# Both conv-FFN layers: other queues for the operand pieces, and layer 1's last six channel tiles by seven products for output tiles 0 to 3

## The chip, the cores and the metric

One core of a Trainium2 chip runs the whole program. Engines named below: TensorE (PE; PEld is its weight load), VectorE (DVE), ScalarE (ACT), GpSimd (POOL) and SyncE (SP, which only issues transfers here). The metric is the device time of one execution in microseconds; several executions are timed and their median is given.

## The reference

Two layers on x of 1024 tokens x 1024 features in float32, then a last RMS norm with a gain. Only the mixer differs between the layers:

```python
for layer in range(2):
    hn = rms_norm(h, norm_mix[layer])
    h = h + (retention_deltanet_mixer if layer == 0 else rglru_mixer)(hn, ...)
    h = h + conv_ffn(rms_norm(h, norm_ffn[layer]), w_up, conv_w, conv_b, w_down)
return rms_norm(h, norm_final)

def conv_ffn(hn, w_up, conv_w, conv_b, w_down):       # D_FF = 2816 = 22 x 128
    up = causal_dwconv(hn @ w_up, conv_w) + conv_b     # 3 taps, 5632 channels
    gate, val = jnp.split(up, 2, axis=-1)
    return (jax.nn.silu(gate) * val) @ w_down
```

## The kernel before, in words

**Precision.** Each float32 factor is split into a high part (rounded on ACT, a CAST) and a low part (the remainder, a subtraction on DVE). A product of a 128x128 weight tile is three matmuls, high x high, high x low, low x high (`mm3`, L319 to L321). Weights come as float32 halves (`raw`, L292) and are split at L272 (ACT) and L273 (DVE).

**H** is the state: eight tiles H[0..7] of 128 features x 1024 tokens, kept in SBUF.

**FFN up** makes 22 hidden channel tiles p = 0 to 21 (`hidden`), a pair of blocks of outputs at a time by seven products instead of eight (`pair_products`; operands o = 0 to 6 are sums and differences of blocks of tokens and channels). **FFN down** uses the same form. Its 22 channel tiles are three sets: c = 0 has tiles 0 to 7, c = 1 has 8 to 15, c = 2 has 16 to 21. In a set the tiles k and k + depth make a pair (depth 4, 4 and 3). A set runs over t = 0 to 3, the pairs (2t, 2t+1) of output tiles, and over the seven products o; one product is depth x 3 matmuls of 512 columns, 12 in sets 0 and 1 and 9 in set 2. `pair_added` adds each product to H on DVE (L820).

**The operands of FFN down.** When tile p is done, `store_parts` writes its share of the seven operands to DRAM. Operands in `whole` are stored already split (to `pf_dram`, high and low, L880; DVE makes the low part at L878). The others go unsplit to `sf_dram` (L881, L906). For the second tile of a pair the first one's blocks are read back first (L894, L895). `load_set(c, o)` brings an operand in: a split one straight to its place in the operand buffers (L914, 2 x depth transfers), an unsplit one to a piece of `room` (R and three t tiles) at L922, depth transfers, after which ACT (L924) and DVE (L925) split it to its place. Every transfer here is 256 KB and is issued by SP, in the order in which the scheduler places them; an engine's queue goes strictly in order, so a transfer that waits for its data holds those behind it. In set 0 of layer 0, operands 0, 1 and 3 are stored split, in the other sets 5 too. The loads of set 0 are issued while tile 21's up products run, the loads of set c + 1 behind the products of t = 3 of set c, as the table `following` (or `plain`) says. Tile 20's hidden work runs beside tile 21's up products; tile 21's runs inside set 0, behind t = 2.

**Layer 1** has only sets 0 and 1. Tiles 16 to 21 are stored split, whole (`lf_dram`), are read back in set 1, and are multiplied plainly in `final`: 8 output tiles x 6 channel tiles x 3 matmuls, over three cuts of the tokens (512, 256 and 256 columns). Their weights are loaded and split once and kept (`load_kept`). After each output tile of a cut its square is added up (L407, L411) for the last norm. The norm of the first 512 tokens runs beside (`norm_beside`: sums through DRAM and POOL to a row in R); those of the second and third cut on TensorE (`norm_tok` L480, POOL's power at L472, `norm_row` L489). `scale` multiplies H with the norm and the gain on DVE (L1044), or on ACT and POOL (L1047), and writes the output.

**Order.** Within each engine instructions stand in an order that a list scheduler made from priorities; PE's order in parts is that of the code (`manual_schedule`). `tc.issue_after(ins)` puts the instructions traced inside it behind `ins` on the engine of `ins`.

Of the kernel before, what the change touches and what calls it, by code (L numbers as in the profile page):

```python
# [103 lines left out]
class Block:  # L104
    def __init__(self, ctx, tc, I, out, stop=None):
# [34 lines left out]
        pad(self.perm, 104, "pad2")  # L140
        self.nhalo = 0
# [45 lines left out]
    def quarter_order(self):  # L187
# [10 lines left out]
        for layer in range(2):  # L198
# [11 lines left out]
            if layer == 0:  # L210
                o += [(("ffn_v0", t), 7) for t in range(4)]
# [601 lines left out]
    def pair_added(self, t):  # L813

        V = self.nc.vector
        h = lambda i, j: self.H[2 * t + i].rearrange("p (h n c) -> p h n c", h=2, n=2)[:, :, j, :]
        to = ((0, 0), (1, 1), (0, 1), (0, 1), (1, 1), (0, 0), (1, 0))

        def sums(o, ps):
            V.tensor_tensor(h(*to[o]), ps.rearrange("p (h c) -> p h c", c=256), h(*to[o]), ALU.add)  # L820
        return sums

    def ffn(self, layer, gain):
        nc, I = self.nc, self.I
        V, A = nc.vector, nc.scalar
        third = gain is not None
        sets = 3 if third else 2
        y_dram = self.tc.dram_tile([NPAIR, P, T], F32, name=f"yf_dram{layer}")
        s_dram = self.tc.dram_tile([sets, 5, 4, P, HALF], F32, name=f"sf_dram{layer}")

        p_dram = self.tc.dram_tile([sets, 4, 4, 2, P, HALF], F32, name=f"pf_dram{layer}")
        if not third:
            l_dram = self.tc.dram_tile([NPAIR - 16, 2, P, T], F32, name=f"lf_dram{layer}")
        depth = lambda c: 4 if c < 2 else 3

        def where(c, o):

            if c == 0 or not third:
                return self.operand(o)
            if c == 1:  # L840
                return self.operand((o + 3) % 7)
            if o < 3:
                i = (20, 14, 26)[o]
                return self.slots1(i, 6).rearrange("p (s n c) -> p n s c", n=2, c=256)
            return self.s2[:, :, 6 * (o - 3):6 * (o - 2), :]
# [14 lines left out]
        whole = [{0: 0, 1: 1, 3: 2}] + 2 * [{0: 0, 1: 1, 3: 2, 5: 3}]  # L860
        room, loads = {}, [0, 0, 0]

        def store_parts(p, y, hi):

            hi = hi.bitcast(F32R)
            lo = self.parts.tile([P, T], F32R, tag="lo", name="lo")
            if p >= 16 and not third:
                self.split_half(y, (hi, lo))
                for e, t in enumerate((hi, lo)):
                    nc.sync.dma_start(l_dram[p - 16, e], f32(t))  # L870
                return
# [4 lines left out]
            def store_split(o, src, at):  # L876
                A.copy(halves(hi[:, at]), src)  # L877
                V.tensor_tensor(halves(lo[:, at]), src, f32(halves(hi[:, at])), ALU.subtract)  # L878
                for e, t in enumerate((hi, lo)):
                    nc.sync.dma_start(p_dram[c, whole[c][o], k % kk, e], f32(t[:, at]))  # L880
            store = lambda o, r: nc.sync.dma_start(s_dram[c, place[o], k % kk], r)  # L881
# [19 lines left out]
            sub(t4, v[:, :, 0], halves(t2))  # L901
            store(6, t4)
            if 5 in whole[c]:
                store_split(5, v[:, :, 0], slice(HALF, T))
            else:
                nc.sync.dma_start(halves(s_dram[c, place[5], k % kk]), v[:, :, 0])  # L906

        def load_set(c, o):
# [7 lines left out]
            if c not in room:  # L916
                ts = [self.R] + [self.t() for _ in range(3)][::-1]
                room[c] = [t[:, i * HALF:(i + 1) * HALF] for i in range(2) for t in ts]
            for k in range(kk):
                r = room[c][loads[c] % 8]  # L920
                loads[c] += 1
                nc.sync.dma_start(r, s_dram[c, place[o], k])  # L922
# [3 lines left out]

        def load_parts(p):
            places = self.place2(p - 16)
            for n in range(2):
                for e in range(2):  # L930
                    nc.sync.dma_start(f32(places[n][e]), l_dram[p - 16, e][:, n * HALF:(n + 1) * HALF])
            return places
# [6 lines left out]
        def hidden(p, tg):  # L939
            tv = conv(NPAIR + p, self.halo[1])  # L940
            V.tensor_tensor(tg, tg, tv, ALU.mult)  # L941
            if (third or p < 16) and p % 8 < depth(p // 8):
# [5 lines left out]
        def after(p, o):  # L948
# [3 lines left out]
            elif o:  # L952
                for q in (0, 1) if o == 1 else (o,):
                    load_set(0, q)
# [13 lines left out]
        ys = {}  # L968
        following = {0: {1: (4, 5), **{o: ((o + 4) % 7,) for o in range(2, 7)}},
                     1: {2: (0,), 3: (1, 2), 4: (3,), 5: (4,), 6: (5, 6)}}  # L970
        plain = {0: {1: (0, 1), **{o: (o,) for o in range(2, 7)}}, 1: {}}
        for c in range(sets):
            done = self.down_steps(gain) if c == 2 else {}
            for t in range(4):
                sums, banks = self.pair_added(t), {}
                key = (f"ffn_w{layer}", c, t) if c < 2 else (f"ffn_v{layer}", t)
                for o in range(7):
                    sums(o, self.pair_product(banks, o, self.quarter(key, o), x=where(c, o)))
                    if t == 3 and c < 2:
# [10 lines left out]
        if not third:  # L990
            self.final([ys[p] for p in range(16, NPAIR)], f"ffn_d{layer}")
# [44 lines left out]
    def final(self, ys, name):  # L1036

        nc = self.nc
        V = nc.vector

# [922 lines left out]
```

## Time and profile before

| what | value |
|---|---|
| median of 3 runs | 2143.78 us (2143.31 to 2144.47) |
| the profiled execution, and its span | 2145.08 us, 2143.2 us |
| TensorE busy | 2127.4 us, 99% |
| VectorE, ScalarE, GpSimd busy | 1722.2, 1077.3, 100.5 us |
| mean granted TensorE clock | 0.999 |
| split operand loads, unsplit operand loads | 136 and 67, 256 KB each, all on SP |
| set 0 of FFN down begins | 984.73 (layer 0), 1912.20 (layer 1) |
| layer 1's plain part begins | 2064.92 |

Times within the profile count from the span's first instruction. A timeline row is: start, length, engine, line, operation, output<-inputs, shape, count, and in brackets what the instruction waited for. In the rows `s` are operand places, `t` and `R` work tiles, `ps` and `pc` banks of PSUM, `h` tiles of H. Matmuls are pipelined, so the distance between starts, not the printed length, is the time of one.

### The profile page before, as it was taken

To read this page: it belongs to the slowest core of one execution; us is meant where nothing else is said; L and a number is where in the kernel's file an instruction comes from. 1 tells how busy PE (TensorE), PEld (TensorE's weight loads), DVE (VectorE), ACT (ScalarE), POOL (GpSimd) and SP (SyncE) were. 2 spreads that over 40 slices of the span, in tenths; PEclk is the share of its full clock that TensorE was granted. 3 is DMA by queue.
4 is the path that set the end of the run, shared out by engine and by line. 5 is a ranking of instruction groups with operands and counts; after the bars stand their busy time and mean duration, and the time that the engine had idled before them with its cause. 6 is when DMAs were issued, how large, how long until landed. Compare 5 with 4: busy or idle time off the path is not lost.

```text
span 2143.2 us, 29749 instructions
## 1 busy us (share of the span) xinstructions
PE 2127.4 (99%) x10648; PEld 1771.9 (83%) x10648; DVE 1722.2 (80%) x2630; ACT 1077.3 (50%) x1750; POOL 100.5 (5%) x115
## 2 busy tenths in 40 slices
PE   9999999999999999999999999999999999999998
PEld 7878888888888888887888888888888888888887
DVE  7995677776998989988868786768999889878645
ACT  6444423135665555555324576756655555554222
POOL 0102122300000000000000000000000000000002
PEclk9999999999999999999999999999999999999999
DMA  5354433543145435448745212142354445375542
GB/s 188 91 170 126 136 94 94 172 142 118 46 172 178 160 137 179 172 172 289 233 161 172 72 57 80 64 158 65 123 186 163 149 151 177 118 262 183 182 169 85
DMA packets 242021, 313.23 MB, mean 146 GB/s; under 512 B 62432, under 2 KB 129424, under 8 KB 241872
## 3 DMA queue, kind: packets, MB, share of 16 engines
q1 hardware_dynamic: 205632, 304.15, 42.5%
q10 hardware_dynamic: 35088, 6.36, 1.5%
q8 instruction: 84, 1.38, 0.3%
q0 software_dynamic: 1152, 0.81, 0.2%
q14 instruction: 65, 0.53, 0.1%
HBM read 215.79 MB, written 95.45 MB: 145 GB/s over the span
## 4 chain that ended last, share of the span: by engine, by line
PE 63%; issue 30%; DVE 3%; DMA 2%; POOL 1%; SPq 0%; ACT 0%; POOLq 0%; DVEq 0%
PE ps L319 19%; PE ps L320 18%; PE ps L321 18%; PE pc L319 1%; PE pc L321 1%; PE pc L320 1%; DMA s<-pf_dram 1%; DMA t<-sf_dram 0%; DVE wlo L273 0%; DVE l L1416 0%; DVE l L1418 0%; DVE h L1387 0%; PE pc L1551 0%; PE ps L1595 0%; PE pc L1663 0%
## 5 line engine op out<-in xcount | busy, mean ns | idle before, releaser
L319 PE MATMUL ps<-s,whi 128*128 128x512 f32 (+1 forms) x2692 | 1049.1, 391 | 1.5 <-DVE h L820 0.9
L320 PE MATMUL ps<-s,whi 128*128 128x512 f32 (+1 forms) x2692 | 1044.1, 388 | 2.1 <-DVE s L925 1.9
L321 PE MATMUL ps<-s,wlo 128*128 128x512 f32 (+1 forms) x2692 | 1042.7, 388 | 0.6 <-DVE wlo L273 0.6
L272 ACT CAST whi<-raw 128x512 fp32r<-128x512 f32 (+2 forms) x616 | 374.1, 613 | 611.9 <-PE ps L320 471.6
L319 PEld LDWEIGHTS ps<-s,whi 128*128 128x128 f32 x2692 | 505.8, 188 | 107.0 <-ACT whi L272 1.6
L320 PEld LDWEIGHTS ps<-s,whi 128*128 128x128 f32 x2692 | 505.9, 188 | 106.1 <-DVE s L925 4.6
L321 PEld LDWEIGHTS ps<-s,wlo 128*128 128x128 f32 x2692 | 505.6, 188 | 104.5 <-DVE wlo L273 1.4
L273 DVE TENSOR_TENSOR wlo<-raw,whi 128x512 fp32r<-128x512 f32 (+2 forms) x616 | 415.0, 680 | 50.8 <-ACT whi L272 42.3
L852 DVE SCALAR_TENSOR_TENSOR t<-halo,cols,t 128x1024 f32<-128x1024 f32 x176 | 221.6, 1281 | 2.4 <-ACT t L850 1.0
L820 DVE TENSOR_TENSOR h<-ps,h 128x512 f32<-128x512 f32 x140 | 96.3, 689 | 75.7 <-PE ps L321 75.5
L810 DVE TENSOR_TENSOR halo<-ps,kept 128x512 f32<-128x512 f32 (+1 forms) x138 | 91.8, 666 | 71.1 <-PE ps L321 70.5
L850 ACT ACTIVATE t<-halo,cols 128x1024 f32<-128x1024 f32 x88 | 109.5, 1247 | 18.0 <-DVE halo L810 9.0
L805 ACT COPY kept<-ps 128x512 f32<-128x512 f32 (+1 forms) x138 | 77.0, 558 | 11.0 <-PE ps L321 9.6
L472 POOL TENSOR_TENSOR rtok<-rtok,npow 128x4 f32<-128x4 f32 (+1 forms) x10 | 9.9, 990 | 1097.2 <-DVE rtok L471 1097.2
L877 ACT CAST t<-t 128x512 fp32r<-128x512 f32 x68 | 41.2, 621 | 39.1 <-DVE t L941 37.1
L941 DVE TENSOR_TENSOR t<-t 128x1024 f32<-128x1024 f32 x44 | 53.6, 1219 | 0.0
L553 DVE TENSOR_TENSOR h<-ps,h 128x512 f32<-128x512 f32 (+1 forms) x48 | 28.6, 599 | 30.6 <-PE ps L321 30.5
L882 DVE TENSOR_TENSOR t<-t 128x512 f32<-128x512 f32 x76 | 52.1, 686 | 0.6 <-DMA sf_dram<-t 0.6
L936 ACT ACTIVATE t<-t 128x1024 f32<-128x1024 f32 x44 | 46.8, 1063 | 10.4 <-DVE t L852 10.3
L407 ACT ACTIVATE t<-h 128x512 f32<-128x512 f32 (+1 forms) x49 | 26.9, 564 | 45.8 <-DVE h L553 43.8
L878 DVE TENSOR_TENSOR lo<-t 128x512 fp32r<-128x512 f32 x68 | 46.7, 686 | 0.0
L294 DVE TENSOR_TENSOR raw<-raw 128x512 f32<-128x512 f32 (+1 forms) x64 | 43.6, 681 | 3.3 <-issue 1.9
(341 smaller groups left out, 2170.7 us busy)
## 6 DMA issues: line engine op xcount, KB each, us to landing
raw<-in_ffn_up_dram SPq DMA_DIRECT2D x176, 256.0 KB, 2.7
s<-pf_dram SPq DMA_DIRECT2D x136, 256.0 KB, 5.2
sf_dram<-t SPq DMA_DIRECT2D x84, 256.0 KB, 2.4
pf_dram<-t SPq DMA_DIRECT2D x68, 256.0 KB, 2.6
pf_dram<-lo SPq DMA_DIRECT2D x68, 256.0 KB, 2.6
t<-sf_dram SPq DMA_DIRECT2D x67, 256.0 KB, 4.8
raw<-in_ffn_w_dram SPq DMA_DIRECT2D x64, 256.0 KB, 3.1
raw<-in_mix_in_dram SPq DMA_DIRECT2D x52, 256.0 KB, 3.0
```

The costliest lines, as they stand in the source:

```text
L272: self.nc.scalar.copy(hi[:, 0:w], raw[:, 0:w])
L273: eng.tensor_tensor(lo[:, 0:w], raw[:, 0:w], f32(hi[:, 0:w]), ALU.subtract)
L319: mm(ps, whi, xhi, start=start, stop=False)
L320: mm(ps, whi, xlo, start=False, stop=False)
L321: mm(ps, wlo, xhi, start=False, stop=stop)
L805: A.copy(kept[o], ps)
L810: V.tensor_tensor(dst(i, j), v(ps), v(kept[k]), ALU.add)
L820: V.tensor_tensor(h(*to[o]), ps.rearrange("p (h c) -> p h c", c=256), h(*to[o]), ALU.add)
L850: A.activation(t, buf[:, 2:2 + T], AF.Identity, scale=w(0), bias=self.col(f"ffn_cb{layer}", tile_i))
L852: V.scalar_tensor_tensor(t, buf[:, 2 + j:2 + j + T], w(j), t, ALU.mult, ALU.add)
L882: sub = lambda out, a, b: V.tensor_tensor(halves(out), a, b, ALU.subtract)
L941: V.tensor_tensor(tg, tg, tv, ALU.mult)
```

## The change

1. **Both layers.** Operand 5 is stored split in every set. Tiles 16 to 21 store, and read back, on POOL's queue instead of SP's. All loads of unsplit operands go on POOL's queue. The difference for operand 6 is written into the tile itself (`t4`), not into a work tile. In set 0 the loads of operands 4 and 6 are traced behind the additions of products 0 and 2 of t = 0, with `issue_after`; before, all of set 0 was loaded from tile 21's up products. The pieces of `room` are used in another order.
2. **Layer 1** now has set 2 for t = 0 and 1: output tiles 0 to 3 get tiles 16 to 21 by seven products (9 matmuls each). A new operand o = 7, the second blocks of tiles 16 to 18, is loaded from `yf_dram`. Operand places of set 1 rotate as in layer 0. `final` multiplies plainly for output tiles 4 to 7 only, from the operands 0, 7, 5 and 3 as they lie. The eight kept weights are loaded and split behind the square of H[1] (`issue_after(squared)`).
3. **The last norm.** Squares of H[0] to H[3] are taken 1024 wide (`final_steps`). The norm of the first 512 tokens goes to TensorE, within the second cut; all its scalings go to DVE, and its output to SP.

The numbers of matmuls change so: 512 columns 54 more, 256 columns 144 fewer.

```diff
-        whole = [{0: 0, 1: 1, 3: 2}] + 2 * [{0: 0, 1: 1, 3: 2, 5: 3}]
+        whole = 3 * [{0: 0, 1: 1, 3: 2, 5: 3}]
...
         def store_parts(p, y, hi):
+            queue = nc.gpsimd if p >= 16 else nc.sync
...
-            if p >= 16 and not third:
-                self.split_half(y, (hi, lo))
-                for e, t in enumerate((hi, lo)):
-                    nc.sync.dma_start(l_dram[p - 16, e], f32(t))
-                return
...
-            t4 = t3
-            nc.sync.dma_start(halves(t3), blocks(y_dram[p - kk])[:, :, 1])
-            nc.sync.dma_start(t2, s_dram[c, place[1], k - kk])
+            t4 = v[:, :, 1]
+            queue.dma_start(halves(t3), blocks(y_dram[p - kk])[:, :, 1])
+            queue.dma_start(t2, s_dram[c, place[1], k - kk])
...
         def load_set(c, o):
...
-                ts = [self.R] + [self.t() for _ in range(3)][::-1]
-                room[c] = [t[:, i * HALF:(i + 1) * HALF] for i in range(2) for t in ts]
+                ts = [self.t() for _ in range(3)]
+                ts = [self.R, ts[1], ts[2], ts[0]]
+                room[c] = [t[:, i * HALF:(i + 1) * HALF] for t in ts for i in range(2)]
             for k in range(kk):
+                queue = nc.gpsimd
...
-                nc.sync.dma_start(r, s_dram[c, place[o], k])
+                if o < 7:
+                    queue.dma_start(r, s_dram[c, place[o], k])
+                else:
+                    queue.dma_start(halves(r), blocks(y_dram[16 + k])[:, :, 1])
...
                 for q in (0, 1) if o == 1 else (o,):
-                    load_set(0, q)
+                    if q not in (4, 6):
+                        load_set(0, q)
...
-        for c in range(sets):
-            done = self.down_steps(gain) if c == 2 else {}
-            for t in range(4):
+        set_at = lambda *at: at in ((0, 0, 0), (0, 0, 2))
+        for c in range(3):
+            done = {}
+            if c == 2:
+                done = self.final_steps() if layer else self.down_steps(gain)
+            for t in range(2 if layer and c == 2 else 4):
...
-                    sums(o, self.pair_product(banks, o, self.quarter(key, o), x=where(c, o)))
+                    last = sums(o, self.pair_product(banks, o, self.quarter(key, o), x=where(c, o)))
+                    if set_at(c, t, o):
+                        with self.tc.issue_after(last.ins):
+                            load_set(0, 4 if o == 0 else 6)
...
+                    if layer and (c, t, o) == (2, 1, 0):
+                        load_set(2, 7)
...
+            for m in range(4, KT):
+                ps = self.pp(both=True)[:, 0:w]
+                for u in range(2):
+                    if (u, m) not in kept:
+                        with self.tc.issue_after(squared):
+                            kept[u, m] = self.load_kept(self.I[name + "ab"[u]][m], places[len(kept)])
...
+        s0 = part(0, 512, more, {4: [self.squares(2)], 5: [self.squares(3)]})
+        s1 = part(512, 256, self.sq[:, 0:HALF],
+                  {4: [lambda: run(self.norm_tok(s0[0]))], 5: [lambda: run(self.norm_row(s0[0], 0))],
+                   6: late(s0, (0, 1), R0), 7: late(s0, (2, 3), R0)})
+        s2 = part(768, 256, self.sq[:, HALF:],
+                  {4: late(s0, (4, 5), R0) + [lambda: run(self.norm_tok(s1[0], 256))],
+                   5: late(s0, (6, 7), R0) + [lambda: run(self.norm_row(s1[0], w=256))],
+                   6: late(s1, range(5), R1), 7: late(s1, range(5, 8), R1)})
```

How the order changes, at three places. SP's queue from tile 20's read-back to the loads of set 0 in layer 0, before (`s_4144` and `s_96` are the two operand buffers):

```order
L895 DMA t<-sf_dram_5167 128x512
L914 DMA s_4144<-pf_dram_5168 128x2x256 x7
L880 DMA pf_dram_5168<-t 128x512
L880 DMA pf_dram_5168<-lo 128x512
L881 DMA sf_dram_5167<-t 128x512 x2
L914 DMA s_4144<-pf_dram_5168 128x2x256
L881 DMA sf_dram_5167<-t 128x512
L914 DMA s_4144<-pf_dram_5168 128x2x256 x7
L922 DMA t<-sf_dram_5167 128x512 x3
L914 DMA s_96<-pf_dram_5168 128x2x256 x8
```

The same place after (the line of the loads is now L906, the buffers `s_4145` and `s_96`):

```order
L292 DMA raw<-in_ffn_w_dram 128x512 x4
L906 DMA s_4145<-pf_dram_5169 128x2x256 x16
L906 DMA s_96<-pf_dram_5169 128x2x256 x16
L292 DMA raw<-in_ffn_w_dram 128x512 x16
L906 DMA s_4145<-pf_dram_5169 128x2x256 x8
```

No store and no unsplit load stands between the 32 loads any more. Those that left SP now stand on POOL's queue, on which there was no operand transfer before. Here it is at tile 20's stores and the first loads of set 0:

```order
L886 DMA t<-yf_dram_5167 128x2x256
L887 DMA t<-sf_dram_5168 128x512
L872 DMA pf_dram_5169<-t 128x512
L873 DMA sf_dram_5168<-t 128x512
L872 DMA pf_dram_5169<-lo 128x512
L873 DMA sf_dram_5168<-t 128x512
L894 DMA sf_dram_5168<-t 256x1x256
L872 DMA pf_dram_5169<-t 128x512
L872 DMA pf_dram_5169<-lo 128x512
L917 DMA t<-sf_dram_5168 128x512 x6
L917 DMA R<-sf_dram_5168 128x512 x2
```

The unsplit loads (L917) stand behind the stores. On DVE, the first additions (L820) of set 0 in layer 0 and the splits between them, before:

```order
L820 TENSOR_TENSOR h_88<-ps,h_88 128x2x256
L273 TENSOR_TENSOR wlo<-raw,whi 128x512
L925 TENSOR_TENSOR s_4144<-t,s_4144 128x2x256 x2
L820 TENSOR_TENSOR h_89<-ps,h_89 128x2x256
L925 TENSOR_TENSOR s_4144<-t,s_4144 128x2x256
L820 TENSOR_TENSOR h_88<-ps,h_88 128x2x256 x2
L925 TENSOR_TENSOR s_96<-t,s_96 128x2x256 x3
L925 TENSOR_TENSOR s_96<-R,s_96 128x2x256
```

and after:

```order
L820 TENSOR_TENSOR h_88<-ps,h_88 128x2x256
L922 TENSOR_TENSOR s_96<-t,s_96 128x2x256 x4
L273 TENSOR_TENSOR wlo<-raw,whi 128x512
L820 TENSOR_TENSOR h_89<-ps,h_89 128x2x256
```

The addition of product 1 (`h_89`) now stands behind four splits, those of operand 4, instead of two.

More of the change, by code (lines that the diff above doesn't have):

```diff
@@ L140, in __init__ @@
         pad(self.perm, 104, "pad2")
+        pad(self.sm, 40, "pad3")
         self.nhalo = 0
@@ L209, in quarter_order @@
             o += [((f"ffn_w{layer}", c, t), 7) for c in range(2) for t in range(4)]
-            if layer == 0:
-                o += [(("ffn_v0", t), 7) for t in range(4)]
+            o += [((f"ffn_v{layer}", t), 7) for t in range(2 if layer else 4)]
         return [(key, j) for key, n in o for j in range(n)]
@@ L825, in ffn @@
         V, A = nc.vector, nc.scalar
-        third = gain is not None
-        sets = 3 if third else 2
         y_dram = self.tc.dram_tile([NPAIR, P, T], F32, name=f"yf_dram{layer}")
[L829 to L833, printed above, removed]
+        s_dram = self.tc.dram_tile([3, 5, 4, P, HALF], F32, name=f"sf_dram{layer}")
+        p_dram = self.tc.dram_tile([3, 4, 4, 2, P, HALF], F32, name=f"pf_dram{layer}")
         depth = lambda c: 4 if c < 2 else 3
         def where(c, o):
-            if c == 0 or not third:
+            if c == 0:
                 return self.operand(o)
@@ L879, in store_split @@
                 for e, t in enumerate((hi, lo)):
-                    nc.sync.dma_start(p_dram[c, whole[c][o], k % kk, e], f32(t[:, at]))
-            store = lambda o, r: nc.sync.dma_start(s_dram[c, place[o], k % kk], r)
+                    queue.dma_start(p_dram[c, whole[c][o], k % kk, e], f32(t[:, at]))
+            store = lambda o, r: queue.dma_start(s_dram[c, place[o], k % kk], r)
             sub = lambda out, a, b: V.tensor_tensor(halves(out), a, b, ALU.subtract)
@@ L900, in store_parts @@
             store(2, t2)
-            sub(t4, v[:, :, 0], halves(t2))
-            store(6, t4)
+            V.tensor_tensor(t4, v[:, :, 0], halves(t2), ALU.subtract)
+            queue.dma_start(halves(s_dram[c, place[6], k % kk]), t4)
             if 5 in whole[c]:
@@ L905, in store_parts @@
             else:
-                nc.sync.dma_start(halves(s_dram[c, place[5], k % kk]), v[:, :, 0])
+                queue.dma_start(halves(s_dram[c, place[5], k % kk]), v[:, :, 0])
         def load_set(c, o):
@@ L941, in hidden @@
             V.tensor_tensor(tg, tg, tv, ALU.mult)
-            if (third or p < 16) and p % 8 < depth(p // 8):
+            if p % 8 < depth(p // 8):
                 nc.sync.dma_start(y_dram[p], tg)
@@ L988, in ffn, with final_steps, square, f @@
                     hidden(NPAIR - 1, gate(NPAIR - 1))
-        if not third:
-            self.final([ys[p] for p in range(16, NPAIR)], f"ffn_d{layer}")
+        if layer:
+            self.final(f"ffn_d{layer}")
+    def final_steps(self):
+        V, A = self.nc.vector, self.nc.scalar
+        self.acc, self.sq = self.t(), self.t()
+        def square(m):
+            def f():
+                if m == 0:
+                    A.activation(self.acc, self.H[m], AF.Square)
+                    return
+                self.squared = A.activation(self.sq, self.H[m], AF.Square)
+                V.tensor_tensor(self.acc, self.acc, self.sq, ALU.add)
+            return f
+        self.squares = square
+        return {(1, 1): [square(0)], (1, 3): [square(1)]}
     def down_steps(self, gain):
@@ L1034, in xplace, with final @@
         return ((0, 1, 2, 5, 3, 4, 6, 7)[k] * 4 + 2 * e) * HALF
-    def final(self, ys, name):
+    def final(self, name):
         nc = self.nc
         V = nc.vector
+        more = self.t()
         def scale(st, sl, k, pr, eng=V, queue=nc.sync):
```

73 lines of the change are left out of this document (35 added, 38 removed).

## The prediction

> **What bounds the kernel now.** I read the page's share of busy time first, then TensorE's waits, then its timeline at each start of a set, then transfers and the tail.
>
> ```profile
> core 0: 2143.2 us, clock 0.999
> PE 2127.4 (99%) x10648; PEld 1771.9 (83%) x10648; DVE 1722.2 (80%) x2630; ACT 1077.3 (50%) x1750; POOL 100.5 (5%) x115
> PE ps L320 <- DVE s L925: 1.9, 6, 0.5
> PE ps L319 <- DVE h L820: 0.9, 1, 0.9
> PE ps L319 <- ACT s L924: 0.6, 1, 0.6
> PE ps L321 <- DVE wlo L273: 0.6, 1, 0.6
> ```
>
> TensorE works 99% of the span at full granted clock. The other four rows are waits (sum, count, longest in us): splits of loaded operands (L924, L925), one addition to H (L820), one weight split. So there are two ways to gain: less to multiply, or fewer of these waits. The times at which matmuls start give both sizes:
>
> ```profile
> 984.73 0.39 PE L319 MATMUL ps<-s,whi 128*128 128x512 f32 x1
> 998.78 0.50 PE L319 MATMUL ps<-s,whi 128*128 128x512 f32 x1 [0.55 <-ACT s L924]
> 1010.16 0.40 PE L319 MATMUL ps<-s,whi 128*128 128x512 f32 x1
> 1151.02 0.39 PE L321 MATMUL ps<-s,wlo 128*128 128x512 f32 x1
> 1152.33 0.47 PE L319 MATMUL ps<-s,whi 128*128 128x512 f32 x1 [0.92 <-DVE h L820]
> 1912.20 0.39 PE L319 MATMUL ps<-s,whi 128*128 128x512 f32 x1
> 2064.92 0.39 PE L319 MATMUL ps<-s,s 128*128 128x512 f32 x1
> 2097.56 0.28 PE L319 MATMUL ps<-s,s 128*128 128x256 f32 x1
> 2121.20 0.28 PE L321 MATMUL ps<-s,s 128*128 128x256 f32 x1
> ```
>
> From 2064.92 to 2097.56 the plain part of layer 1 issues 8 output tiles x 6 channel tiles x 3 = 144 matmuls of 512 columns: 32.64/144 = 0.2267 us each. From there 198 of 256 columns take 23.64: 0.12 each. Layer 1's sets 0 and 1 (672 matmuls, 152.3 us) take 152.7, so layer 1 loses 0.4 to waits. Layer 0 is different: set 0 starts at 984.73, and 87 matmuls (19.7) have taken 25.43 at 1010.16: 5.7 us lost. Its change from set 1 to set 2 (1151.02 to 1152.33) costs 1.31 for one pitch: 1.1 lost.
>
> **Why set 0 of layer 0 waits.** Set 0 loads 24 split operand pieces (pf) and 16 unsplit ones (sf), 256 KB each, all through SP. Windows: length, TensorE busy, its weight loads, DVE, ACT, POOL, clock, DMA share, GB/s.
>
> ```profile
> s<-pf_dram SPq DMA_DIRECT2D x136, 256.0 KB, 5.2
> t<-sf_dram SPq DMA_DIRECT2D x67, 256.0 KB, 4.8
> 966.34 0.52 SPq L914 DMA_DIRECT2D s<-pf_dram  x1
> 977.69 0.53 SPq L914 DMA_DIRECT2D s<-pf_dram  x1
> 980.39 0.32 SPq L881 DMA_DIRECT2D sf_dram<-t  x1
> 980.00:985.00 5.00, 5.00 (x24) 4.14 (x23) 4.06 (x7) 1.47 (x3) 0.00 (x0) 1.00 0.80 261
> 985.00:990.00 5.00, 4.88 (x22) 3.72 (x20) 1.98 (x3) 1.48 (x3) 0.00 (x0) 1.00 0.95 298
> 995.00:1000.00 5.00, 4.12 (x17) 2.70 (x16) 2.15 (x4) 1.83 (x3) 0.00 (x0) 1.00 1.07 400
> 1900.00:1905.00 5.00, 5.00 (x24) 4.14 (x23) 5.00 (x8) 3.12 (x5) 0.00 (x0) 1.00 1.04 382
> 1920.00:1925.00 5.00, 5.00 (x23) 4.14 (x23) 4.37 (x7) 4.21 (x7) 0.00 (x0) 1.00 1.04 388
> 1134.89 9.45 SPq L914 DMA_DIRECT2D s<-pf_dram  x13
> 1144.50 0.48 SPq L922 DMA_DIRECT2D R<-sf_dram  x1
> 1149.89 0.62 ACT L924 CAST s<-R 128x512 fp32r<-128x512 f32 x1 [2.19 <-DMA R<-sf_dram]
> L878 DVE TENSOR_TENSOR lo<-t 128x512 fp32r<-128x512 f32 x68 | 46.7, 686 | 0.0
> ```
>
> The first load is issued 18.4 us ahead of set 0, but tile 20's stores stand between the loads in SP's order: at 977.69 a load goes, then SP is held for 2.7 us until a store (980.39) has its data. The transfers run at 261 to 298 GB/s where they later reach 400; layer 1, whose tiles 16 to 21 are stored in another way, is at 382 to 388 already. At set 1 to 2 a load of R goes only at 1144.50, behind 13 loads in a row, and ACT waits 2.19 us for it. The last two rows give what splitting a loaded piece takes: 0.62 on ACT, then 0.69 on DVE (the row is that of a split of the same shape).
>
> **The change, part by part.**
>
> *TensorE's work, layer 1.* Added: 2 pairs x 7 products x 9 = 126 matmuls of 512 columns. Plain part: 4 output tiles instead of 8, so 72 fewer of 512 and 144 fewer of 256. 54 x 0.2267 = +12.2; 144 x 0.12 = −17.3; together **−5.1**.
>
> *The norm of the first 512 tokens* moves from POOL and DRAM to TensorE. Layer 0 shows such a norm:
>
> ```profile
> 1208.42 0.65 PE L480 MATMUL pc<-t,ones 128*32 128x128 f32 x16
> 1208.99 0.50 PE L319 MATMUL ps<-s,whi 128*128 128x512 f32 x1
> 1209.80 1.05 PE L489 MATMUL pc<-ident,rtok 128*128 128x128 f32 x8
> 1210.60 0.47 PE L319 MATMUL ps<-s,whi 128*128 128x512 f32 x1
> ```
>
> 0.57 + 0.80 = **+1.4**. POOL's small step between them (L472) is covered by the six channel tiles' products of one output tile, 18 x 0.12 = 2.2 us; without that cover TensorE waits for it.
>
> *Set 0, layer 0.* Operand 5 is now stored split: 4 more transfers in, and no ACT and DVE splits for it. SP issues four weight loads and then 32 pf loads with no store between; tile 20's stores and all sf loads go on POOL's queue. DMA then limits: 32 pf + 12 sf + 9 of tile 20 = 53, two of which (sf) can go early: 51 x 262 KB = 13.4 MB, at 385 GB/s (between 382 and 388) 34.7 us. From 18.4 before the set's start that ends 16.3 after it, and about 2 later it has landed: 18.3. Product 6 begins at 6 x 12 x 0.2267 = 16.3, so its first piece, split included (0.62 + 0.69), is late by a little, its last by some 2.4. I leave 2.7 of the 5.7, with small waits for weights: **−3.0**. Bounds: 0 (nothing gained) to −5.4 (the transfers were slow only for the held queue). I stay near the middle because the volume grows by 4 while the gaps that close, 980 to 990, are worth 10 x (385 − 280)/385 = 2.7 us, about four transfers.
>
> The loads of operands 4 and 6 move behind the first and third addition of the set, so DVE's four splits for operand 4 (4 x 0.7 = 2.8) stand between two additions, and the addition of product 1 comes late by up to that. Two more products (5.4 us) pass before its bank is needed: nothing, at most 1.
>
> *Set 0, layer 1.* The same 51 instead of 40 and four stores' worth, 44: 7 more, 7 x 0.68 = 4.8, where the set so far loses 0.4. Its windows are full at 1900 and at 1920, so there is little slack; but the loads of 4 and 5 come in two queues, and operand 5 no longer needs splits. By the sum above the end is again 2.4 late: **+2.0**, between −0.4 (slack takes it) and +4.8.
>
> *Set 1 to 2, layer 0.* The sf loads no longer stand behind the 13 pf loads: **−1.1** (to 0, if POOL's queue has them late).
>
> *Set 1 to 2, layer 1,* is new: 24 pf, 9 sf, then 3 more for operand 7. DVE splits six sf pieces (6 x 0.7 = 4.2) ahead of the first addition of set 2. The nearest row is layer 0's own such place, 0.9 for a late addition: **+1.0**, between 0 and 3.
>
> *Kept weights.* Eight loads, split behind the square of H1, three products (3 x 9 x 0.2267 = 6.1 us) before the plain part: the first two tiles need about 2.6 of ACT and DVE. Nothing; 1.3 if the pair comes last on a busy DVE.
>
> *Tail.* DVE scales all eight 512-wide tiles, POOL none.
>
> ```profile
> 2115.23 0.75 DVE h L1044
> 2117.34 3.48 DVE L1044 SCALAR_TENSOR_TENSOR h<-h,cols,R 128x512 f32<-128x512 f32 x2
> 2117.09 4.87 POOL L1047 TENSOR_TENSOR h<-h,R 128x512 f32<-128x512 f32 x3
> 2122.43 1.07 DVE L553 TENSOR_TENSOR h<-ps,h 128x256 f32<-128x256 f32 x3
> 2137.30 2.44 DVE L1044 SCALAR_TENSOR_TENSOR h<-h,cols,pc 128x256 f32<-128x256 f32 x6 [1.98 <-ACT R L1079]
> ```
>
> Alone such a scaling takes 0.75; beside POOL's it took 1.74. Four more at 0.75 are 3.0, four others fall from up to 1.74 to 0.75. In the two 256-column cuts (8.6 us each) DVE then has 8 additions (1.07/3 = 0.36), 8 squares' additions (the same), 8 scalings of 512 and 8 of 256 (2.44/6 = 0.41): 2.9 + 2.9 + 6.0 + 3.3 = 15.1 in 17.2 plus the norms' small steps, about 1.5: it keeps up with little to spare. **0**; if they take 1.74 each, 8 more, of which about 1 is slack: +7.
>
> Sum: −5.1 + 1.4 − 3.0 − 1.1 + 2.0 + 1.0 + 0 = **−4.8**. The profiled execution took 2145.08 (span 2143.2 and 1.9 around it); 2140.3 is forecast for it. The median of the runs lies 1.3 below that execution, 2143.78, so the forecast is **2139.0**, 0.22% faster. 0.2% is 4.3 us, about what a measurement of this kernel can tell from no change.
>
> **Rivals.**
>
> *All waits go.* SP was only held up, and bandwidth is no limit: −5.1 + 1.4 − 5.4 − 1.1 − 0.4 = −10.6: **2133.2**. For it: 400 GB/s in 995 to 1000, and pieces can start 18 us ahead. Against: layer 1's full windows.
>
> *Volume takes it.* Layer 0 keeps its 5.7 and layer 1 gets 4.8: −5.1 + 1.4 − 1.1 + 4.8 + 1.0 (up to 3) = +1.0 to +3: **2144.8** to 2146.8. For it: 7 to 11 more transfers where DMA is full.
>
> *POOL's queue is too slow (slower).* POOL issues 21 of the 53 (12 sf, 9 of tile 20) in 34.7 us, so up to 1.65 us each it costs nothing.
>
> ```profile
> L1437 POOL DMA_DIRECT2D l<-t_dram x32: 551/551/621, 174.6 to 224.1; - x32
> 212.70:215.40 2.70, 2.70 (x14) 2.21 (x13) 2.51 (x3) 1.19 (x2) 2.21 (x4) 1.00 0.40 105
> ```
>
> POOL's only loads in this trace are small: 0.55 each (2.21 for 4) beside a DVE that is 93% busy (2.51 of 2.70). A 256 KB load isn't shown. From 2.0 us each, 42 us in all, both layers lose 7 more, and the change is slower: −4.8 + 14 = +9.2, **2153**. By the row it is nearest to, 0.55, it doesn't happen.
> The Trainium skill speaks for this rival ("SBUF — State Buffer", section "A bandwidth-pool intuition that's wrong (but worth ruling out)"): a transfer issued from GpSimd took about 620 ns alone and about 3100 ns beside a VectorE copy, because its descriptors wait for the shared port. By 3.1 us the 21 would take 65 us and the estimate would be 2139 + 2 x 30 = 2199. The trace so far doesn't agree (0.55 beside a busy DVE), and the page's section "Who interferes with whom" exempts two-operand tensor operations, which are what DVE mostly runs here.
>
> *DVE ends the tail.* +7 on −4.8: **2146.0**. Against: the 0.75 row.
>
> **How the numbers follow.** Forecast 0.38 (half of it beyond 0.2% faster), all waits go 0.27, volume 0.18, POOL's queue 0.10, tail 0.07. Faster: 0.19 + 0.27 = 0.46, with a little of the others 0.47; slower: POOL's 0.10 and the upper ends of volume and tail, 0.03 = 0.13; same 0.40. The range goes from the second case, 2133, to the upper end of the volume case, 2147, which leaves out POOL's queue and both outer ends, under 2 in 10. The forecast's own range is 2136 to 2142.5.
>
> **What would show it.** Matmuls: 512-column ones up by 54, 256-column down by 144. Start of set 0 to the 88th matmul: 22 to 23 us in both layers (19.7 if all waits go, 25 if volume takes it). POOL's issues about 0.6 to 1 us each; 2 and more with TensorE waiting on splits of sf pieces says that the queue is the bound. In layer 1's last third the norm of 512 tokens on TensorE, two pieces of near 0.57 and 0.80; no L820 wait over 0.5 at layer 0's set 2. Wrong: a new wait in layer 1's set 2 over 3 us, or last scalings of 512 after the last matmul.

## The result, and the profile after

The changed kernel takes 2172.16 us (median of 4 runs, 2170.36 to 2174.32) against 2143.55 before: ratio 1.0134, 95% interval 1.0116 to 1.0151. It is 28.6 us slower; the forecast was 2139.0 (2133 to 2147). The profiled execution took 2173.34, span 2171.5, so 28.3 more than before.

The page and TensorE's waits after (sum, count, longest in us):

```profile
core 0: 2171.5 us, clock 0.993
PE 2136.9 (98%) x10582; PEld 1771.6 (82%) x10582; DVE 1740.7 (80%) x2672; ACT 1081.0 (50%) x1763; POOL 179.1 (8%) x260
PE ps L319 <- DVE h L820: 16.1, 6, 5.0
PE ps L320 <- DMA s<-pf_dram: 3.2, 5, 1.6
PE ps L319 <- DMA s<-pf_dram: 2.8, 3, 1.3
```

TensorE has 66 instructions fewer (54 − 144 and 24 of the norm), as the change says. But it now waits 16.1 us for additions to H, where it waited 0.9 for one, and 6.0 for split operands, and its mean clock has fallen from 0.999 to 0.993. Its timeline at the first places:

```profile
984.16 0.39 PE L319 MATMUL ps<-s,whi 128*128 128x512 f32 x1
994.17 0.77 PE L319 MATMUL ps<-s,whi 128*128 128x512 f32 x1 [4.41 <-DVE h L820]
994.74 0.63 PE L320 MATMUL ps<-s,whi 128*128 128x512 f32 x1
995.16 0.63 PE L321 MATMUL ps<-s,wlo 128*128 128x512 f32 x1
1009.96 0.77 PE L319 MATMUL ps<-s,whi 128*128 128x512 f32 x1 [2.07 <-DVE h L820]
1934.02 0.77 PE L319 MATMUL ps<-s,whi 128*128 128x512 f32 x1 [5.05 <-DVE h L820]
```

Set 0 begins at 984.16. After two products (24 x 0.2267 = 5.44) TensorE stops at 989.6 until 994.17, and after the stop the matmuls start 0.42 to 0.43 apart instead of 0.2267. The windows show why (clock is the third column from the end):

```profile
985.00:990.00 5.00, 4.76 (x22) 3.60 (x20) 0.69 (x1) 1.18 (x2) 2.55 (x5) 1.00 1.06 404
990.00:995.00 5.00, 0.83 (x2) 0.77 (x3) 2.96 (x5) 4.59 (x10) 1.08 (x2) 0.78 1.04 406
995.00:1000.00 5.00, 5.00 (x14) 3.90 (x14) 4.25 (x7) 3.81 (x5) 0.00 (x0) 0.54 1.08 386
```

The granted clock falls to half after the wait. So each long wait is paid a second time.

What each place loses, worked out in every kernel's timeline as the distance between starts beyond 0.2267 per matmul, added up over the place (us; L0 and L1 are the layers, "0-1" the stretch from set 0 to set 1; under 0.4 is shown as 0):

| kernel | L0 set 0 | L0 0-1 | L0 1-2 | L1 set 0 | L1 0-1 | L1 1-2 |
|---|---|---|---|---|---|---|
| before | 5.5 | 0 | 1.1 | 0.4 | 0 | no set 2 |
| changed | 11.1 | 6.9 | 1.1 | 9.5 | 6.4 | 4.1 |
| e6, layer 1's part alone | 4.7 | 0 | 0.8 | 5.6 | 0.6 | 1.5 |
| e20, that with tile 20 in set 1 | 0 | 0 | 0 | 0 | 0 | 1.4 |

Against before the changed kernel loses 5.6 + 6.9 + 0 + 9.1 + 6.4 + 4.1 = 32.1 more there; with 3.7 less to multiply that is 28.4 of the 28.3 measured. Of the 39.1 lost in all, 22.5 are waits that the timeline names; about 11 are 53 matmuls that wait for nothing but run while the granted clock is at half and start some 0.42 apart; the rest, about 5, is the restart after each wait and gaps too short to be listed.

**The chain of the first stall.** POOL, ACT and DVE of the changed kernel in layer 0, in order of time:

```profile
980.08 0.56 POOL L872 DMA_DIRECT2D pf_dram<-lo  x1 [2.41 <-issue]
983.24 3.36 POOL L917 DMA_DIRECT2D t<-sf_dram  x6 [2.60 <-DMA sf_dram<-t]
988.60 0.62 ACT L921 CAST s<-t 128x512 fp32r<-128x512 f32 x1 [6.57 <-DMA t<-sf_dram]
989.25 1.53 DVE L922 TENSOR_TENSOR s<-t,s 128x512 fp32r<-128x512 f32 x2 [6.32 <-ACT s L921]
991.08 0.62 ACT L921 CAST s<-t 128x512 fp32r<-128x512 f32 x1 [0.20 <-DMA t<-sf_dram]
992.08 0.62 ACT L272 CAST whi<-raw 128x512 fp32r<-128x512 f32 x1
992.73 0.69 DVE L273 TENSOR_TENSOR wlo<-raw,whi 128x512 fp32r<-128x512 f32 x1 [1.95 <-ACT whi L272]
993.34 0.68 DVE L820 TENSOR_TENSOR h<-ps,h 128x512 f32<-128x512 f32 x1
```

The first unsplit loads into work tiles stand on POOL behind tile 20's last store and go at 983.24, 0.9 ahead of the set, since those tiles come free when the stores out of them have landed. Issuing is quick (3.36/6 = 0.56 each). ACT meanwhile stands at their casts, four in a row from 988.60; the cast of the next weights (L272) waits behind them, DVE's half of it (L273) behind that, and the addition of product 0 behind that, at 993.34. Product 2 accumulates in the bank that this addition must first read (`BANK = "ACACABA"`), so TensorE stops.

What product 2 reads is not what stops it. The loads at 983.24 bring the last two pieces of operand 2 and then operand 4; the first two pieces of operand 2 lie in R and were split at 975.95 and 976.56. The last two are split by 990.78 (the row of 989.25), and TensorE, coming to product 2 at 989.60, would reach the very last at 989.60 + 9 x 0.2267 = 991.64. The next two casts belong to operand 4, which is needed two products later, and the cast of the weights stands behind them.

**The second stall** has another cause. SP issues 32 split loads in a row, and the next weights only after them:

```profile
965.77 32.83 SPq L906 DMA_DIRECT2D s<-pf_dram  x32
998.80 14.37 SPq L292 DMA_DIRECT2D raw<-in_ffn_w_dram  x8
1004.26 0.62 ACT L272 CAST whi<-raw 128x512 fp32r<-128x512 f32 x1 [4.93 <-DMA raw<-in_ffn_w_dram]
```

The cast of weights waits 4.93 us, and again an addition behind it.

**Set 0 to 1**, which had no wait. SP before, then SP and POOL after:

```profile
1050.94 16.00 SPq L914 DMA_DIRECT2D s<-pf_dram  x24
1068.97 5.25 SPq L914 DMA_DIRECT2D s<-pf_dram  x8
1077.71 0.33 SPq L922 DMA_DIRECT2D R<-sf_dram  x1
```

```profile
1055.80 28.45 SPq L906 DMA_DIRECT2D s<-pf_dram  x32
1061.18 1.07 POOL L917 DMA_DIRECT2D t<-sf_dram  x2 [1.73 <-DVE s L922]
1071.22 1.07 POOL L917 DMA_DIRECT2D t<-sf_dram  x2 [1.34 <-DVE s L922]
1077.43 0.50 PE L319 MATMUL ps<-s,whi 128*128 128x512 f32 x1 [1.26 <-DMA s<-pf_dram]
```

Before, set 2's unsplit loads (from 1077.71) stood on SP behind set 1's 32 split ones. On POOL nothing holds them but a free piece of the room: eight of them, from 1061.18 to 1071.22, go over 80 us ahead of their set, and set 1's loads take 28.45 us instead of 23.3.

### The profile page after: what moved, and what is told of

It is laid out like the page before. It is cut to its first block, busy times and chain, and to the rows that moved or that the text cites. A ratio compares the mean times of both kernels' runs of the same rounds, so it can differ in the third digit from the quotient of the medians.

```text
span 2171.5 us, 29938 instructions
## 1 busy us (share of the span) xinstructions
PE 2136.9 (98%) x10582; PEld 1771.6 (82%) x10582; DVE 1740.7 (80%) x2672; ACT 1081.0 (50%) x1763; POOL 179.1 (8%) x260
## 4 chain that ended last, share of the span: by engine, by line
PE 88%; issue 6%; DMA 3%; DVE 2%; POOL 0%; ACT 0%; SPq 0%; POOLq 0%; DVEq 0%; ACTq 0%
PE ps L319 26%; PE ps L320 26%; PE ps L321 26%; DMA s<-pf_dram 2%; PE pc L319 1%; PE pc L320 1%; PE pc L321 1%; DMA raw<-in_ffn_w_dram 0%; PE ps L1678 0%; PE ps L1680 0%; PE ps L1679 0%; DMA raw<-in_mix_in_dram 0%; PE pc L489 0%; PE pc L1586 0%; PE ps L1630 0%
## 5 line engine op out<-in xcount | busy, mean ns | idle before, releaser
L319 PE MATMUL ps<-s,whi 128*128 128x512 f32 (+1 forms) x2734 | 1071.0, 392 | 19.4 <-DVE h L820 16.1
L320 PE MATMUL ps<-s,whi 128*128 128x512 f32 (+1 forms) x2734 | 1065.1, 390 | 3.5 <-DMA s<-pf_dram 3.2
L321 PE MATMUL ps<-s,wlo 128*128 128x512 f32 (+1 forms) x2734 | 1062.8, 389 | 0.0
L272 ACT CAST whi<-raw 128x512 fp32r<-128x512 f32 (+2 forms) x630 | 382.0, 611 | 662.5 <-PE ps L320 533.5
L319 PEld LDWEIGHTS ps<-s,whi 128*128 128x128 f32 x2734 | 515.8, 189 | 132.5 <-ACT s L921 10.2
L320 PEld LDWEIGHTS ps<-s,whi 128*128 128x128 f32 x2734 | 516.3, 189 | 111.3 <-DMA s<-pf_dram 8.3
L321 PEld LDWEIGHTS ps<-s,wlo 128*128 128x128 f32 x2734 | 515.9, 189 | 105.2
L273 DVE TENSOR_TENSOR wlo<-raw,whi 128x512 fp32r<-128x512 f32 (+2 forms) x630 | 423.0, 677 | 55.9 <-ACT whi L272 43.4
L820 DVE TENSOR_TENSOR h<-ps,h 128x512 f32<-128x512 f32 x154 | 106.0, 689 | 88.3 <-PE ps L321 88.0
L869 ACT CAST t<-t 128x512 fp32r<-128x512 f32 x88 | 52.4, 619 | 41.7 <-DVE t L931 39.7
L870 DVE TENSOR_TENSOR lo<-t 128x512 fp32r<-128x512 f32 x88 | 60.4, 686 | 0.0
L872 POOL DMA_DIRECT2D pf_dram<-t x24 | 13.5, 562 | 553.3 <-ACT t L869 553.0
L472 POOL TENSOR_TENSOR rtok<-rtok,npow 128x4 f32<-128x4 f32 (+1 forms) x11 | 11.1, 1010 | 579.7 <-DVE rtok L471 579.7
L379 DVE TENSOR_TENSOR halo<-ps,R 128x512 f32<-128x512 f32 x36 | 24.6, 686 | 27.1 <-PE ps L321 25.2
```

The source lines that it names most:

```text
L272: self.nc.scalar.copy(hi[:, 0:w], raw[:, 0:w])
L273: eng.tensor_tensor(lo[:, 0:w], raw[:, 0:w], f32(hi[:, 0:w]), ALU.subtract)
L319: mm(ps, whi, xhi, start=start, stop=False)
L320: mm(ps, whi, xlo, start=False, stop=False)
L321: mm(ps, wlo, xhi, start=False, stop=stop)
L820: return V.tensor_tensor(h(*to[o]), ps.rearrange("p (h c) -> p h c", c=256), h(*to[o]), ALU.add)
```

## The experiments

The changed kernel's edits are undone or added one by one; times are medians, ratios against the kernel before (2144.5 to 2144.9, timed beside each) with 95% intervals. All edits of queues are these two lines of `load_set` and `store_parts`:

```diff
-                queue = nc.gpsimd                                  # loads
+                queue = nc.sync
-            queue = nc.gpsimd if p >= 16 else nc.sync              # stores, tiles 16 to 21
+            queue = nc.sync
```

**e1, loads back on SP** (the first edit).

> The changed kernel with the loads of unsplit operands back on SP's queue; the stores of tiles 16 to 21 stay on POOL's. Theory Q (the unsplit loads on a queue of their own cost the time: they share bandwidth with the split loads that are needed first, and the order of DVE and ACT places their splits ahead of the additions): the four stalls at the additions of set 0 and the waits for split operands at set 0 to 1 go, in both layers, and of the 28 us about 24 come back: 2145 to 2150. Theory S (the stores on POOL hold the loads behind them): little comes back, over 2160. Theory V (the four more transfers of operand 5 cost it): set 0 still loses 5 to 9 us in each layer, 2158 to 2165.

It takes 2151.8 us, ratio 1.0031 (1.0016 to 1.0047), 1.8 above the range of theory Q. 20 us come back. The waits at set 0 to 1 are gone in both layers, and layer 1's set 2 loses 0.7 instead of 4.1; set 0 still loses 7.4 and 9.0, now with a wait of 3.0 and 2.7 for a cast of a loaded piece and one of 1.7 and 2.2 for an addition. Theory Q holds for all places but set 0.

**e2, stores back on SP** (the second edit).

> The changed kernel with the stores and read-backs of tiles 16 to 21 back on SP's queue; the unsplit loads stay on POOL's. Theory Q: the waits for split operands at set 0 to 1 stay as they are (about 6.5 us in each layer), set 0 gets a little better, 2162 to 2175. Theory S: set 0's stalls go, about 15 us come back, 2157 or less. Theory V: as it was, 2168 to 2175.

It takes 2165.3 us, ratio 1.0097 (1.0077 to 1.0117). Set 0 to 1 loses 7.4 and 6.3 as before the edit; set 0 loses 6.1 in both layers and now waits for split loads, 1.5 at the longest, with no wait for an addition. So the stall of 4.4 and 5.1 us for an addition came only with stores and loads together on POOL's queue; with one of the two on SP set 0 still loses 6 to 9.

**e3, both back on SP.**

> The changed kernel with both back on SP's queue: what is left of the change is operand 5 stored split, operands 4 and 6 loaded behind additions, and layer 1's set 2 with the new tail. Theories Q and S: 2139 to 2146. Theory V: set 0 loses 5 us or more in each layer, 2148 to 2155.

It takes 2150.2 us, ratio 1.0026 (1.0015 to 1.0036): above the range of Q and S, within that of V. Set 0 loses 6.2 and 6.9, in many small waits and at full clock.

**e6, layer 1's part alone** (both queues, operand 5 of set 0 unsplit, the room's order, operand 6's place and the loads of 4 and 6 as before).

> The kernel before with only layer 1's part of the change (set 2 by seven products for output tiles 0 to 3, kept weights later, the last norm on TensorE); queues, operand 5 and the loads of set 0 as before. By the sum of the prediction TensorE has 3.7 us less, and a new place from set 1 to set 2 costs 0 to 3: 2139 to 2143. A theory that layer 1's new set itself costs the time expects 2148 or more.

It takes 2146.5 us, ratio 1.0011 (1.0001 to 1.002), between the two ranges: a part that takes 3.7 us from TensorE makes the kernel no faster. Layer 1's set 0 now loses 5.6 where it lost 0.4.

**e4, both on SP, loads of 4 and 6 early.**

```diff
-                    if q not in (4, 6):
-                        load_set(0, q)
+                    load_set(0, q)
-        set_at = lambda *at: at in ((0, 0, 0), (0, 0, 2))
+        set_at = lambda *at: False
```

> Both queues back on SP and operands 4 and 6 of set 0 loaded from tile 21's products, as before the change; left are operand 5 stored split, the order of the room's pieces and layer 1's part. Beside the kernel with both on SP (2150.2) this undoes only the loads behind additions; beside layer 1's part alone (2146.5) it adds only operand 5 stored split. If the four more transfers cost the 3.6 us between those, about 2150; if the loads behind additions do, about 2146.5.

It takes 2153.9 us, ratio 1.0042 (1.0026 to 1.0058): neither value. Set 0 loses 9.0 and 7.9, one wait of 2.7 for a split among it. So putting the loads of 4 and 6 behind additions helps, by 3.7 against e3, and does not cost.

**e14, layer 1's part and operand 5 split**

```diff
-        whole = [{0: 0, 1: 1, 3: 2}] + 2 * [{0: 0, 1: 1, 3: 2, 5: 3}]
+        whole = 3 * [{0: 0, 1: 1, 3: 2, 5: 3}]
```

on e6.

> The kernel with only layer 1's part of the change (2146.5), and operand 5 of set 0 stored split in both layers; the room's order, the place of operand 6's difference and all queues as before. If the four more transfers of each set 0 cost time by themselves, 4 x 0.67 = 2.7 us a layer: 2150 to 2153. If the room's order or the difference in place made the 7 us of the kernel with both on SP and early loads, 2145 to 2148.

It takes 2151.0 us, ratio 1.0031 (1.002 to 1.0041): 4.5 more than e6 for eight more loads, in the range of the volume theory. Its place is not wholly that of the theory. Of the 3.7 between the profiled spans 1.8 stand in the places of the table (6.5 and 1.6 in layer 0, 6.2 and 0.7 in layer 1). Set beside e6 matmul by matmul, e14 is 0.7 behind within the first 60 us, far ahead of both FFNs; set 0 adds 2.2 in layer 0 and 1.0 in layer 1, where the theory expects 2.7 each, set 1 to 2 adds 0.8 in layer 0, and layer 1's places behind set 0 take 1.3 off.

**e7, operand 2 behind the first addition too.**

```diff
-                    if q not in (4, 6):
+                    if q not in (2, 4, 6):
...
-                            load_set(0, 4 if o == 0 else 6)
+                            for q in (2, 4) if o == 0 else (6,):
+                                load_set(0, q)
```

> The changed kernel, queues as changed, but operand 2 of set 0 is also traced behind the first addition, so that its splits on DVE stand behind that addition and not ahead of it. If the order on DVE makes the stall (an addition that waits behind splits whose loads are late), the first wait of TensorE in set 0, 4.4 us in layer 0 and 5.1 in layer 1, falls to the lateness of operand 2 itself, under 3 us, and the half clock after it is shorter: 2160 to 2168. If the late load alone makes it, whichever instruction waits, the first stall stays 4 to 6 us and the time 2168 to 2176.

It takes 2174.1 us, ratio 1.0139 (1.0119 to 1.0159). The first wait stays 4.26, though on DVE the addition now stands ahead of the splits:

```profile
981.23 0.63 ACT L272 CAST whi<-raw 128x512 fp32r<-128x512 f32 x1 [2.09 <-PE ps L320]
988.29 0.62 ACT L921 CAST s<-t 128x512 fp32r<-128x512 f32 x1 [6.43 <-DMA t<-sf_dram]
991.74 0.62 ACT L272 CAST whi<-raw 128x512 fp32r<-128x512 f32 x1
992.39 0.69 DVE L273 TENSOR_TENSOR wlo<-raw,whi 128x512 fp32r<-128x512 f32 x1 [9.65 <-ACT whi L272]
993.00 0.68 DVE L820 TENSOR_TENSOR h<-ps,h 128x512 f32<-128x512 f32 x1
```

DVE waits 9.65 us for ACT, whose weight cast stands behind the four casts of late loads. So what stands ahead of the addition on DVE is not what holds it here: `issue_after` orders DVE alone, and ACT's order stays.

**e8, set 1's unsplit loads small**, and **e9, set 2's**. A small load brings 32 of the 512 columns of its piece, 1/16 of the bytes; the rest is left out, so these two kernels measure time alone:

```diff
+                if c == 1:                                          # e9: c == 2 and o < 7
+                    queue.dma_start(r[:, 0:32], s_dram[c, place[o], k][:, 0:32])
...
```

> The changed kernel, but each unsplit load of set 1 on POOL's queue brings 32 of its 512 columns (the split repeats them; the rest of these operands is left out). Same queue, same number of transfers, 1/16 of the bytes. If the waits for split operands at set 0 to 1 come from shared bandwidth, they go: from 6.9 and 6.4 us to under 1.5 in each layer, 2158 to 2163. If they come from the second queue as such, or from SP's own order, they stay and the time is 2168 to 2174.

It takes 2172.6 us, ratio 1.0132 (1.0112 to 1.0152): 5.2 and 5.4 left at set 0 to 1. By its own ranges this spoke for the queue as such, but it took away the wrong bytes: most of set 1's loads go earlier, and only four of the twelve in that stretch are its own.

> The changed kernel, but each unsplit load of set 2 on POOL's queue brings 32 of its 512 columns (the split repeats them; the rest of these operands is left out). In the changed kernel's trace eight of set 2's nine such loads run 80 us ahead of their set, at set 0 to 1. If these bytes make the split loads of set 1 late, the waits there fall from 6.9 and 6.4 us to 2 to 4 in each layer (the four loads of set 1 that were small in the earlier run took 1.7 and 1.0 off), and the time is 2162 to 2168. If the queue as such does it, they stay over 6 and the time is 2169 to 2174. Set 0 loses 11 and 9.5 us either way.

It takes 2162.3 us, ratio 1.0082 (1.0062 to 1.0102): 1.6 and 1.5 left, of 6.9 and 6.4. Same queue, same number of transfers: what makes set 1's operands late is bandwidth taken by set 2's loads, far ahead of their need.

**e10, e6 with the stores on POOL.**

> The kernel with only layer 1's part of the change (2146.5), and of the change of queues only the stores and read-backs of tiles 16 to 21 on POOL; all loads on SP, operand 5 of set 0 unsplit, set 0 loaded from tile 21's products. If SP held behind tile 20's stores makes the loss of set 0 (4.7 and 5.6 us), it falls to about 2 in each layer: 2139 to 2142. If the volume of transfers makes it, or if DVE and ACT then wait at other places, it stays: 2145 to 2150.

It takes 2150.1 us, ratio 1.0024 (1.0014 to 1.0034). Set 0 loses 5.2 and 6.9, at other instructions: waits of 1.4 and 2.2 for DVE. Freeing SP is not enough.

**e11, e6 without tile 20's transfers.**

```diff
                 for e, t in enumerate((hi, lo)):
-                    queue.dma_start(p_dram[...], f32(t[:, at]))
+                    if p != 20:
+                        queue.dma_start(p_dram[...], f32(t[:, at]))
...
```

> The kernel with only layer 1's part of the change (2146.5), without the read-backs and stores of tile 20 in both layers (set 2 takes tile 19's operands in their place; tile 20's are left out; sums and splits are still made). If set 0 loses 4.7 and 5.6 us because tile 20's transfers hold SP and the work tiles that the unsplit loads go to, both losses fall under 2: 2137 to 2141. If 24 split and 16 unsplit loads are too much by themselves, they stay over 4: 2145 to 2147.

It takes 2136.4 us, ratio 0.9963 (0.9949 to 0.9977), 0.6 below the first range. Set 0 loses nothing in either layer. 24 split and 16 unsplit loads are not too much; tile 20's seven stores and two read-backs among them are.

**e16, e6 with tile 20's share later**, behind the first pair of set 0; **e17**, the same on the kernel before, layer 0 only.

```diff
+            if p % 8 < depth(p // 8) or p == 20:
                 nc.sync.dma_start(y_dram[p], tg)
-            store_parts(p, tg, tv)
+            if p != 20:
+                store_parts(p, tg, tv)
...
+                if (c, t) == (0, 0):                                # e20 and e21: (1, 1)
+                    y20, hi20 = self.t(), self.t()
+                    nc.sync.dma_start(y20, y_dram[20])
+                    store_parts(20, y20, hi20)
```

> The kernel with only layer 1's part of the change (2146.5), with tile 20's share of set 2's operands made later: tile 20 is stored whole beside tile 21's products, read back behind the first pair of set 0, and only then read, split and stored as before (the result is the full one; 512 KB more are stored and 512 KB more loaded). If tile 20's transfers at that place are what set 0 loses to (without them it lost nothing, 2136.4), the losses of 4.7 and 5.6 us fall under 2 in each layer: 2136 to 2140, faster than the kernel before (2144.5). If the store of 512 KB holds SP and the work tiles as well, they stay over 4: 2144 to 2148.

> The kernel before, with tile 20's share of set 2's operands made later in layer 0 alone (layer 1 has no such share). If tile 20's transfers make layer 0's loss of 5.5 us, it falls under 2: 2139 to 2142. If not, 2143 to 2146.

They take 2145.3 us, ratio 1.0004 (0.9995 to 1.0013), and 2143.3, 0.9993 (0.9984 to 1.0002): both in the range that stood for no gain. Yet nothing is lost any more up to 1009, 25 us into set 0; in e16 2.3, 1.1 and 1.6 us stand later, up to the start of set 1, at weight splits and additions. There the moved work met a DVE that was full (5.00 of 5 us busy from 1005 to 1010 and from 1015 to 1025); whether that is the reason, e20 asks.

**e18, the changed kernel with tile 20 later** (the same edit).

> The changed kernel, queues as changed, with tile 20's share of set 2's operands made later in both layers. If set 0's stalls come from unsplit loads that stand behind tile 20's stores on POOL's queue (and from the casts on ACT that wait for them), they go: 11 and 9.5 us fall to under 4 each, 2155 to 2160, and what is left is the waits at set 0 to 1. If POOL's queue makes the loads late without tile 20 too, set 0 still loses 6 or more in each layer: 2164 to 2173.

It takes 2166.9 us, ratio 1.0105 (1.0087 to 1.0123), in the second range, though not for its reason. The first stall is gone (2.1 left of some 7 in layer 0), but another comes at 1007: TensorE waits 4.25 for a weight cast, SP having issued weights only behind the 32 split loads.

**e20, e6 with tile 20's share in set 1**, where DVE has room (2.5 to 4.3 of 5 us busy from 1100 to 1125); **e21**, the kernel before with that alone.

> The kernel with only layer 1's part of the change, with tile 20's share of set 2's operands made in set 1 (behind its second pair) and no longer in set 0, where the version before this one moved the loss to (2.3, 1.1 and 1.6 us in layer 0, waits for weight splits and additions while DVE is full). If tile 20's place is the cause, set 0 loses under 1 in each layer and the new waits go: 2136 to 2140, faster than the kernel before. If tile 20's work costs 4 us wherever it stands, 2143 to 2147.

> The kernel before, with layer 0's tile 20 moved in the same way and nothing else of the change. By its place: 2138 to 2140. If the work costs as much wherever it stands: 2142 to 2145. Beside the other kernel of this call it tells what layer 1's seven products bring once set 0 does not pay for them: 3.7 less TensorE work and up to 1.5 for the new place from set 1 to set 2, so the other should be 1 to 4 us faster.

They take 2137.4 us, ratio 0.9967 (0.9955 to 0.9979), and 2139.4, 0.9977 (0.9968 to 0.9987). Both are faster than the kernel before, and e20 than both kernels, by 7.1 and 34.8 us. TensorE's waits of e20, and the windows at the place of the first stall:

```profile
core 0: 2134.4 us, clock 0.999
PE ps L319 <- DVE h L820: 0.9, 2, 0.8
985.00:990.00 5.00, 5.00 (x24) 4.14 (x23) 3.42 (x7) 2.16 (x5) 0.00 (x0) 1.00 1.03 360
990.00:995.00 5.00, 5.00 (x24) 4.14 (x23) 3.66 (x7) 3.73 (x6) 0.00 (x0) 1.00 1.02 386
```

The transfers run at 360 to 386 GB/s and TensorE does not stop. Layer 1's part is worth 2.0 us there: 3.7 by the sum, less the 1.4 that its set 2 still loses.

## Why the prediction was wrong

Between the forecast of −4.8 us and the measured +28.3 lie 33.1: set 0 of both layers has 15.7 of them, the stretch from set 0 to 1, for which the sum had no term, 13.3, and the stretch from set 1 to 2 has 4.2.

**Right.** TensorE's work: 3.7 less; the matmul counts, and the 2.0 of e20 against e21, agree. The tail: from the start of the last matmul of the products to the end 10.3 us, 10.0 before. POOL's price: 0.54 to 0.66 us (median 0.54) for a 256 KB load, also beside a busy DVE, far under the 1.65 from which the rival was to decide. That rival had the right side and the right queue by luck, since the price that it rested on didn't come. The 3.1 us per transfer that the prediction took from the Trainium skill ("SBUF — State Buffer", section "A bandwidth-pool intuition that's wrong (but worth ruling out)") are not seen either.

**Set 0, layer 0: −3.0 forecast, +5.6 measured.** The step that failed is the sum of transfers: it let POOL's loads begin 18 us ahead and asked only when the last one lands. Two go early, into R; the others begin 0.9 ahead at the most (983.24), since they stand behind tile 20's stores and need the tiles that these stores read; when tile 20's share is made later, the first stall goes (e18). Volume does count in part, as e14 shows, but it was not what stopped TensorE there. (By its own figures the sum's last piece would be split at 18.3 + 1.3 = 19.6, where product 6 reaches it at 18.4: 1.2 late, not 2.4.)

**"Nothing, at most 1" for the late additions.** It said that two more products pass before the bank is needed. Products 0 and 2 share a bank, so it is one, 2.7 us. And it read DVE's order from the first addition on: two splits stand ahead of that, and ACT's order, in which weight casts stand behind casts of late loads, was not read at all; that order makes the wait (e7).

**Set 0 to 1: no term; 6.9 and 6.4 measured.** "All sf loads go on POOL's queue" was costed only where they were late before, at set 1 to 2. That a queue of its own lets loads run ahead of more urgent ones was missed; e9 shows it.

**Set 1 to 2, layer 0: −1.1 forecast, 0 measured** (1.1 lost as before): other waits took its place, the longest 0.4 for a weight cast. **Layer 1: +1.0 forecast, +4.1**, one wait of 2.36 and the half clock after it; with loads on SP it is 0.7 to 1.5.

**Set 0, layer 1: +2.0 forecast, +9.1.** 5.2 come with layer 1's part alone (e6): tiles 16 to 21 take the paired way, and tile 20's transfers, which cost layer 0 its 5.5, now cost layer 1 as much (e11). The prediction counted them as volume alone, 7 transfers more. In the changed kernel it is the same chain as in layer 0: POOL's loads go at 1923.07, 0.3 us ahead of the set, and TensorE waits 5.05 us for the addition.

**The clock: no term; about 11 of the 28 us.** In the changed kernel half the clock follows waits of 2.07, 2.36, 4.41 and 5.05 us, for 3.4 or 6.8 us each, and the shorter waits at set 0 to 1, for 3.4. The Trainium skill, "TensorE: Matmul & The Clock Gate", Part 1, has the rule: an idle TensorE falls to half rate, judged in windows of about 3.4 us that run freely. The spacing of 0.42 to 0.43 and the 3.4 us agree; that it takes an idle window of 3.4 us first doesn't, since 2.07 was enough here.

**Open.** How e4's 2.9 us beyond e14 divide between the room's order and operand 6's place was not tried. What in tile 20's transfers costs set 0 its 5 us, their bytes or the work tiles that they keep, is not separated: e10 shows only that it is not SP's queue alone, and e11 and e20 take both away. That DVE was the reason in e16 is argued from its busy time; e20 moved the work to another place altogether.

## What to carry to other kernels

A queue is also a priority: loads that stand behind urgent ones in one queue can run ahead of them on a queue of their own, and take their bandwidth (e9), so ask for each moved transfer what held it back and whether that was useful. When loads may be late, read the in-order streams of every engine that handles them: one late cast holds the weights behind it, and a wait of 2 us can be paid again in clock. A store phase that falls on a load phase is best moved to a quiet stretch, even for an extra round trip through DRAM: that, and not the seven products, made most of the gain here.

## What the runs showed of the hardware

Over all runs the granted clock halved in or right after every wait of TensorE of 2.68 us or more; between 1.8 and 2.5 it halved after some (1.83 in e18, 2.07 in the changed kernel) and not after others (2.07 in e7, 2.49 in e8). Shorter waits that come close together did it too: 1.21 and 1.26 at 1074 to 1078 in the changed kernel, and waits of 1.3 to 1.6 at set 0 to 1 in e2, e7 and e8. Within the products each time lasted 3.41 or 6.83 us. The 66 loads of 256 KB issue from POOL in 0.54 to 0.66 us, beside an idle DVE and beside a busy one. SP's and POOL's queues together moved 386 to 406 GB/s (985 to 1000, changed kernel), about what SP's alone did (400, kernel before).
